# Ten SwiGLU pairs from seven products, with the sums of weights made by GpSimd beside them

## The chip, the cores and the metric

The kernel runs on one core of a Trainium2 chip. The metric is the device time of one execution in microseconds: 818.55 is the median of three runs (817.93 to 819.12). Five engines work side by side, each on its own list of instructions in a fixed order: TensorE (PE, with its weight loads as PEld), VectorE (DVE), ScalarE (ACT), GpSimd (POOL) and SyncE (SP). SP issues nearly all the loads and stores here.

## The reference

A decoder block on 512 tokens of width 1024, all in float32. What matters here:

```python
h = rmsnorm(x, norm1_g)
z = h @ w_in + b_in                     # 1024 -> 2048 + 1280 + 1280 + 1024 + 1024
...                                     # conv branch y_a, gated recurrence y_b
m = sigmoid(z_ga) * y_a + sigmoid(z_gb) * y_b
x = x + m @ w_mix_out
h = rmsnorm(x, norm2_g)
x = x + (silu(h @ ffn_w1) * (h @ ffn_w3)) @ ffn_w2      # width 2816 between
return rmsnorm(x, norm_f_g)
```

The recurrence has two block-diagonal products (lru_wa and lru_wx, 16 heads of 80 channels).

## The kernel before

Activations lie with channels on the 128 partitions and tokens (512) along the row. To keep float32 accuracy on TensorE, each operand is split into a high and a low part, and a product is three matmuls: high x high, high x low, low x high. For a weight chunk of 128x1024 the split is a copy on ScalarE (line 118) and a subtraction (line 114): on GpSimd for the input stage's weights, on VectorE for all later ones.

**Weights.** `wchunk` lists the chunks in the order in which they are used; `emit_chunk` issues a chunk's load into one of four raw tiles and its split into one of five hl tiles; `weights(key, ahead)` emits up to four chunks beyond the one asked for. So a split can begin when the product five chunks earlier has ended.

**Stages.** Input stage (products z, gates g, the two branches; GpSimd splits its weights), products yb and ya, the mixing product (mxr), norm 2, the SwiGLU stage (f and fr), the last product (or) with the final norm. The Tile framework orders each engine's instructions when the kernel is compiled, from the order of the program text; inside `manual_schedule` the order of the text is kept. `issue_after(ins)` puts a block's instructions on `ins`'s engine behind `ins`.

**Products from seven.** A product that is cut into 2x2 quarters on each side can be made from seven quarter products instead of eight, from sums of the inputs' quarters and of the weights' quarters (b11, b12, b21, b22 and the sums t1 = b12 - b11, t2 = b22 - b12 + b11, t3 = b22 - b12, t4 = b21 - t2). `Sevenfold` does so for the mixing product and the last product. In the SwiGLU stage a pair k is the output tiles k and k + 11 of both w1 and w3. Before, pairs 2 to 6 (`SEVEN`) come from seven products (`ffn_seven`, 168 matmuls of 256 columns), the other six are plain (96 matmuls of 512).

**Sums of weights.** For pairs 2 to 6, `make_f_sums` runs in the input stage: 20 blocks, each with four loads, four GpSimd instructions of 128x256 and four stores to device memory. The SwiGLU stage loads the sums back. For the last product `make_sums` runs in the SwiGLU stage on VectorE: 11 blocks, each with two loads, four VectorE instructions of 128x512 and four stores (`out_sums`).

**Beside norm 2.** The first plain pair (tiles 0 and 11) is begun on the first 256 tokens while the second 256 are normalised, then finished on the second. `turn_half` makes h2's halves: transposes on TensorE, the high part on ScalarE, the low part on VectorE. `f_inputs` makes the seven products' inputs from h2: eight additions high + low on GpSimd, sixteen sums of 128x256 and eight splits on VectorE. `pair` does the same for the last product's input, after each pair k.

**Gates and ext.** A gate chunk j loads pieces of lru_wa and lru_wx, one DMA for each piece of each. The channels of a head that lie in the neighbouring tile come by way of `ext`: parts of xb's split tiles, copied by DMA (`ext_in`, line 698).

Of the kernel before, what the change touches and what calls it, by code (L numbers as in the profile page):

```python
# [44 lines left out]
SEVEN = (2, 3, 4, 5, 6)  # L45
SUMS_AT, SUMS_STEP, SUMS_LAG, STORE_LAG = 4, 3, 2, 5
# [35 lines left out]
def tile_block(ctx, tc, a, out):  # L82
# [53 lines left out]
    def emit_chunk():  # L136
# [3 lines left out]
        raw = raws.tile([P, 1024], F32, tag="raw", name=f"raw_{key}")  # L140
        rv = raw[:, :n]
        if callable(src):
# [3 lines left out]
        if where == "hl":  # L146
# [30 lines left out]

    gate_view = lambda v: v.rearrange("p (g e n) -> p g e n", g=2, e=2)

    def gate_chunk(j):  # L180
        main, runs, blocks = pieces[j % 5]

        def load(raw):
            pool_e.memset(raw[:, :512], 0.0)
            v = gate_view(raw[:, :512])
            for gi, name in enumerate(("lru_wa", "lru_wx")):
                for ei, blk in ((0, main), (1, blocks)):
                    for r, nr, c, ncol, h, hr, hc in blk:
                        nc.sync.dma_start(v[r : r + nr, gi, ei, c : c + ncol], a[name][0, h + 8 * (j // 5), hr : hr + nr, hc : hc + ncol])
# [34 lines left out]
    dram = ctx.enter_context(tc.tile_pool(name="dram", bufs=1, space=bass.MemoryType.DRAM))  # L224

    class Quartered:
        def __init__(self, name, w, kh, lo, parts=()):
# [3 lines left out]
            self.sums = {(n, k): dram.tile([P, T], F32, tag=f"{name}{n}_{k}", name=f"{name}{n}_{k}") for n in ("t1", "t2", "t3", "t4") if n not in parts for k in range(kh)}  # L231
            self.at = {}

            def quarter(n, k):
                if n[0] == "t":
                    return self.sums[n, k][:, :]
                i, h = int(n[1]) - 1, int(n[2]) - 1
                return w[:, k + kh * i, h * T : (h + 1) * T]
# [11 lines left out]
            for p_ in (("b11", "t1", "b21"), ("t2", "t3", "b22"), ("t4",)):  # L250
                p_ = [n for n in p_ if n not in parts]
                for k in range(kh):
                    if len(p_) % 2 and k % 2 == 0:
                        chunk(f"{p_[-1]}_{k}", [(p_[-1], i) for i in (k, k + 1) if i < kh])
                    if len(p_) > 1:
                        chunk(f"{p_[0]}_{k}", [(n, k) for n in p_[:2]])

# [19 lines left out]
        def make_sums(self, k):  # L277
# [8 lines left out]
            for n, v in (("t1", q12), ("t2", q11), ("t3", q22), ("t4", q21)):  # L286
                if n in self.parts:
                    self.parts[n][k] = split(f"{self.name}{n}{k}", v, vec)
                else:
                    nc.sync.dma_start(self.sums[n, k][:, :], v)  # L290
# [7 lines left out]
    f_sums = {(n, k): dram.tile([P, 1024], F32, tag=f"f{n}_{k}", name=f"f{n}_{k}") for k in SEVEN for n in ("t1", "t2", "t3", "t4")}  # L298

# [5 lines left out]
    def f_chunk(n, k):  # L305
        def load(raw_t):
            if n[0] == "t":
                nc.sync.dma_start(raw_t, f_sums[n, k][:, :])
            else:
                for i, w_ in enumerate((w1, w3)):  # L310
                    nc.sync.dma_start(raw_t[:, i * T : (i + 1) * T].rearrange("p (k n) -> p k n", k=4), f_quarter(n, k, w_, 0, 4))

        wchunk(f"f{n}_{k}", load, 8, P, lo=vec)

    def make_f_sums():

        todo = [(k, i, c) for k in SEVEN for i in range(2) for c in (0, 2)]
        sums_due, stores_due = [], []  # L320
        n = 0
        while todo or sums_due or stores_due:
            if stores_due and emitted[0] >= stores_due[0][0]:
                stores_due.pop(0)[1]()
            if sums_due and n >= sums_due[0][0]:
                sums_due.pop(0)[1]()
            if todo and n >= SUMS_AT and (n - SUMS_AT) % SUMS_STEP == 0:
                k, i, c = todo.pop(0)
                raw = wsums.tile([P, 1024], F32, tag="wsum", name=f"fws{k}_{i}_{c}")
                q = [raw[:, 256 * m : 256 * m + 256] for m in range(4)]  # L330
                with tc.issue_after(newest["load"]):
                    for m, v in zip(("b11", "b12", "b21", "b22"), q):
                        nc.sync.dma_start(v.rearrange("p (k n) -> p k n", k=2), f_quarter(m, k, (w1, w3)[i], c, c + 2))

                def sums(q=q, k=k, at=T * i + P * c):
                    q11, q12, q21, q22 = q
# [6 lines left out]
                    def stores():  # L343
                        with tc.issue_after(newest["load"]):
                            for m, v in (("t1", q12), ("t2", q11), ("t3", q22), ("t4", q21)):
                                nc.sync.dma_start(f_sums[m, k][:, at : at + 256], v)

                    stores_due.append((emitted[0] + STORE_LAG, stores))

                sums_due.append((n + SUMS_LAG, sums))  # L350
            n += 1
            yield

    for k in range(KF):
        if k in SEVEN:
            for n in ("b11", "b21", "b22", "t2", "t1", "t3", "t4"):
                f_chunk(n, k)
        else:
            for j in (k, k + KF):
                wchunk(f"f1_{j}", w1[:, :, j * P : (j + 1) * P], ND, P, lo=vec)  # L360
                wchunk(f"f3_{j}", w3[:, :, j * P : (j + 1) * P], ND, P, lo=vec)
    outq = Quartered("o", a["ffn_w2"][0].rearrange("(k p) n -> p k n", p=P), NF // 2, vec)
# [147 lines left out]
    with tc.manual_schedule(engines={ET.PE, ET.Activation, ET.DVE, ET.SP}):  # L510
# [248 lines left out]
    f_sums_steps = make_f_sums()  # L759
    for kind, j in ORDER:  # L760
        next(f_sums_steps, None)
# [20 lines left out]
    for j in range(8):  # L782
# [5 lines left out]
        next(f_sums_steps, None)  # L788
# [4 lines left out]
    for _ in f_sums_steps:  # L793
# [366 lines left out]
```

## Time and profile before

| | |
|---|---|
| median of 3 runs | 818.55 us |
| span of the profiled execution | 817.8 us |
| granted TensorE clock, mean | 0.997 |
| TensorE's last matmul of the SwiGLU stage begins | 703.6 us |
| HBM | read 127.13 MB, written 28.31 MB |

The span is from the first to the last instruction of one profiled execution; its times are in microseconds from the span's start. In a group's row stand the line, the engine, the operation, the output and inputs by the program's names, the shape and the count, then busy us and the mean ns of one, then the engine's idle time before them and what ended it. In a timeline's row stand start, length, engine, line and what it does. A matmul's length is longer than its share of time, since matmuls overlap; what one costs is read from the starts of a run of them.

### The profile page before, as it was taken

How to read it: one execution, taken by the hardware profiler on the slowest of the kernel's cores; microseconds unless marked ns; L12 is line 12 of the kernel's file. 1: busy time of each engine (PE TensorE's matmuls, PEld its weight loads, DVE VectorE, ACT ScalarE, POOL GpSimd, SP SyncE). 2: the span in 40 equal slices, each digit the busy share in tenths (PEclk: the TensorE clock that was granted, in tenths of full speed). 3: DMA queues.
4: the chain of work that ended last, by engine and by line, in shares of the span. 5: the costliest groups of instructions: out<-in, count | busy, mean ns of one | idle time of the engine just before them, and what ended most of it. 6: DMA issues, size and time to landing. Idle time of an engine off the chain costs nothing.

```text
span 817.8 us, 11826 instructions
## 1 busy us (share of the span) xinstructions
PE 800.2 (98%) x4110; PEld 685.3 (84%) x4110; DVE 654.9 (80%) x1018; ACT 448.4 (55%) x633; POOL 225.3 (28%) x172
## 2 busy tenths in 40 slices
PE   8999999899999999999999999999999999999996
PEld 7988888678888888888888898999998888788885
DVE  4699899989989988787878869787877565779556
ACT  7546585977668855553336455364644222466443
POOL 3575766866765854000000042000000000000000
PEclk9999999999999999999999999999999999999999
DMA  6746466477675753456838524788787887796552
GB/s 195 206 127 163 128 172 201 125 191 201 180 207 166 210 177 113 126 169 217 262 117 245 155 92 149 249 251 268 227 238 207 272 266 266 277 316 206 180 168 103
DMA packets 189551, 159.25 MB, mean 195 GB/s; under 512 B 14407, under 2 KB 157171, under 8 KB 189491
## 3 DMA queue, kind: packets, MB, share of 16 engines
q1 hardware_dynamic: 189491, 158.50, 63.5%
q8 instruction: 32, 0.52, 0.3%
q14 instruction: 28, 0.23, 0.1%
HBM read 127.13 MB, written 28.31 MB: 190 GB/s over the span
## 4 chain that ended last, share of the span: by engine, by line
PE 68%; DVE 12%; DMA 10%; SPq 3%; ACT 3%; issue 2%; POOL 2%; DVEq 0%; POOLq 0%; ACTq 0%
PE z L438 24%; PE or L841 12%; PE fr L1017 9%; PE yb L438 7%; PE ya L438 5%; PE mxr L841 5%; PE f L438 4%; DVE cv L597 3%; DMA ows<-in_ffn_w_dram 3%; DMA raw_in<-in_w_in_dram 2%; DMA ot<-ows 2%; PE g L718 1%; DVE hl_f L114 1%; POOL hl_in L114 1%; DVE ows L114 1%
## 5 line engine op out<-in xcount | busy, mean ns | idle before, releaser
L597 DVE SCALAR_TENSOR_TENSOR cv<-u,par,cv 128x511 f32<-128x511 f32 (+16 forms) x240 | 162.4, 730 | 2.4 <-ACT cv L594 2.2
L114 POOL TENSOR_TENSOR hl_in<-raw_in,hl_in 128x1024 fp32r<-128x1024 f32 x52 | 125.6, 2422 | 81.2 <-ACT hl_in L118 80.3
L118 ACT CAST hl_in<-raw_in 128x1024 fp32r<-128x1024 f32 x52 | 54.2, 1043 | 10.9 <-PE z L438 6.5
L114 POOL TENSOR_TENSOR fws<-fws 128x256 f32<-128x256 f32 x60 | 47.8, 799 | 5.0 <-DMA fws<-in_ffn_w_dram 2.3
L991 POOL TENSOR_TENSOR hf<-h20h,h20l 128x512 f32<-128x512 f32 x1 | 1.3, 1271 | 163.5 <-DVE h20l L482 163.5
L118 ACT CAST hl_f<-raw_f 128x1024 fp32r<-128x1024 f32 x24 | 25.1, 1051 | 36.3 <-DMA raw_f<-in_ffn_w_dram 14.9
L438 PE MATMUL z<-h10h,hl_in 128*128 128x512 f32 (+1 forms) x112 | 42.6, 382 | 1.1 <-DVE h10l L482 0.6
L438 PE MATMUL z<-h11h,hl_in 128*128 128x512 f32 (+1 forms) x112 | 41.7, 374 | 0.0
L438 PE MATMUL z<-h16h,hl_in 128*128 128x512 f32 (+1 forms) x112 | 41.7, 374 | 0.0
L438 PE MATMUL z<-h13h,hl_in 128*128 128x512 f32 (+1 forms) x112 | 41.7, 374 | 0.0
L438 PE MATMUL z<-h14h,hl_in 128*128 128x512 f32 (+1 forms) x112 | 41.7, 374 | 0.0
L438 PE MATMUL z<-h15h,hl_in 128*128 128x512 f32 (+1 forms) x112 | 41.7, 374 | 0.0
L438 PE MATMUL z<-h17h,hl_in 128*128 128x512 f32 (+1 forms) x112 | 41.7, 374 | 0.0
L438 PE MATMUL z<-h12h,hl_in 128*128 128x512 f32 (+1 forms) x112 | 41.7, 374 | 0.0
L114 DVE TENSOR_TENSOR hl_ob<-raw_ob,hl_ob 128x1024 fp32r<-128x1024 f32 (+1 forms) x23 | 26.9, 1176 | 17.8 <-ACT hl_ob L118 17.7
L118 ACT CAST hl_ob<-raw_ob 128x1024 fp32r<-128x1024 f32 (+1 forms) x23 | 23.3, 1015 | 31.7 <-PE or L841 12.0
L114 DVE TENSOR_TENSOR hl_f<-raw_f,hl_f 128x1024 fp32r<-128x1024 f32 x24 | 32.9, 1380 | 9.5 <-ACT hl_f L118 9.4
L114 DVE TENSOR_TENSOR ows<-ows,ows 128x512 f32<-128x512 f32 x22 | 15.2, 690 | 19.6 <-DMA ows<-in_ffn_w_dram 15.3
L1017 PE MATMUL fr<-hs_0h,hl_ft 128*128 128x256 f32 x160 | 29.7, 284 | 0.9 <-ACT c L1029 0.9
L114 DVE TENSOR_TENSOR hl_ft<-raw_ft,hl_ft 128x1024 fp32r<-128x1024 f32 x20 | 24.4, 1219 | 5.3 <-ACT hl_ft L118 5.3
L114 DVE TENSOR_TENSOR hl_ot<-raw_ot,hl_ot 128x1024 fp32r<-128x1024 f32 (+1 forms) x17 | 20.1, 1190 | 10.6 <-ACT hl_ot L118 10.2
L438 PEld LDWEIGHTS z<-h10h,hl_in 128*128 128x128 f32 x112 | 21.4, 191 | 5.8 <-DVE h10l L482 0.9
(903 smaller groups left out, 2602.5 us busy)
## 6 DMA issues: line engine op xcount, KB each, us to landing
raw_in<-in_w_in_dram SPq DMA_DIRECT2D x52, 512.0 KB
raw_f<-in_ffn_w_dram SPq DMA_DIRECT2D x24, 512.0 KB
ows<-in_ffn_w_dram SPq DMA_DIRECT2D x22, 512.0 KB
ot<-ows SPq DMA_DIRECT2D x44, 256.0 KB
fws<-in_ffn_w_dram SPq DMA_DIRECT2D x80, 128.0 KB
ft<-fws SPq DMA_DIRECT2D x80, 128.0 KB
raw_ft<-ft SPq DMA_DIRECT2D x20, 512.0 KB
raw_ob<-in_ffn_w_dram SPq DMA_DIRECT2D x33, 256.0 KB
```

The lines of the kernel that those rows point to most:

```text
L114: return eng.tensor_tensor(out=o, in0=x, in1=y, op=ALU.subtract)
L118: copy(h, full)
L438: pe.matmul(ps, l, r, start=i == 0, stop=i == n - 1)
L597: vec.scalar_tensor_tensor(out=acc[c][:, s:], in0=u[c][:, : T - s], scalar=dw(c, s), in1=acc[c][:, s:], op0=ALU.mult, op1=ALU.add)
L718: pe.matmul(ps, l, r, start=k == 0, stop=k == len(mms) - 1)
L841: pe.matmul(banks[i], l_[:, ts], r_, start=start and n == 0, stop=stop and n == 2, skip_group_check=again)
L991: pool_e.tensor_tensor(out=v, in0=h2p[c][0].bitcast(F32), in1=h2p[c][1].bitcast(F32), op=ALU.add)
L1017: pe.matmul(ps[:, HALVES[i]], lw[:, 4 * i + c, :], rx_, start=not (again or i or c or m), stop=bool(i and c == 3 and m == 2), skip_group_c ...
```

## The change

- In the SwiGLU stage, pair 0 is plain and pairs 1 to 10 come from seven products. Each loads its four quarters (b11, b21 into the raw tiles, b12, b22 into the two wsums tiles), and GpSimd makes t1 to t4 in place, four subtractions of 128x1024: t1 when its chunk is emitted, t2, t3 and t4 after b22's split. The sums take no way through device memory.
- Beside norm 2, pairs 1 and 2 are begun: their first two products need only the first 256 tokens. They are finished after pair 0; for that b11, b12 and b21 are loaded again.
- `f_inputs` makes its eight additions on VectorE instead of GpSimd.
- The last product's sums of weights are made in the input stage by GpSimd: 22 blocks, each with two loads, four instructions of 128x256 and one store. `out_sums` is gone from the SwiGLU stage.
- `pair` of the last product is run for pairs 0 to 3 in the SwiGLU stage, and for 4 to 10 three steps ahead in the first loop of `Sevenfold.run`.
- The gate weights are first copied, device memory to device memory, into one tensor with lru_wa and lru_wx side by side; a gate chunk's piece of both then comes in one DMA.
- ext for gate tiles 0 and 5 is made by two ScalarE copies and one VectorE subtraction from xb instead of by DMA from the split parts.

```diff
-SEVEN = (2, 3, 4, 5, 6)
-SUMS_AT, SUMS_STEP, SUMS_LAG, STORE_LAG = 4, 3, 2, 5
+PLAIN, FIRST = 0, (1, 2)
+EARLY_SUMS, SUMS_AHEAD = 4, 3
+SUMS_AT, SUMS_STEP, SUMS_LAG, STORE_LAG = 4, 3, 2, 4
...
+    def load_gates():
+        for gi, name in enumerate(("lru_wa", "lru_wx")):
+            nc.sync.dma_start(gate_rows[:, gi, :], a[name][0].rearrange("h r n -> (h r) n"))
...
-            for gi, name in enumerate(("lru_wa", "lru_wx")):
-                for ei, blk in ((0, main), (1, blocks)):
-                    for r, nr, c, ncol, h, hr, hc in blk:
-                        nc.sync.dma_start(v[r : r + nr, gi, ei, c : c + ncol], a[name][0, h + 8 * (j // 5), hr : hr + nr, hc : hc + ncol])
+            for ei, blk in ((0, main), (1, blocks)):
+                for r, nr, c, ncol, h, hr, hc in blk:
+                    at_ = HB * (h + 8 * (j // 5)) + hr
+                    nc.sync.dma_start(v[r : r + nr, :, ei, c : c + ncol], gate_rows[at_ : at_ + nr, :, hc : hc + ncol])
...
+    def f_load(n, k):
+        p_, tag = (wsums, "wsum") if n in ("b12", "b22") else (raws, "raw")
+        raw = p_.tile([P, 1024], F32, tag=tag, name=f"raw_f{n}_{k}")
+        for i, w_ in enumerate((w1, w3)):
+            nc.sync.dma_start(raw[:, i * T : (i + 1) * T].rearrange("p (k n) -> p k n", k=4), f_quarter(n, k, w_, 0, 4))
+        f_raw[n, k] = raw
+        return raw
+
+    def f_sum(n, k):
+
+        q11, q12, q21, q22 = (f_raw.get((m, k)) for m in ("b11", "b12", "b21", "b22"))
+        o, x, y = {"t1": (q12, q12, q11), "t2": (q22, q22, q12), "t3": (q11, q22, q11), "t4": (q21, q21, q22)}[n]
+        sub(pool_e, o, x, y)
+        f_raw[n, k] = o
+
+    F_ORDER = ("b11", "b21", "t1", "b22", "t2", "t3", "t4")
+    F_LOADS = {"b11": ("b11", "b12"), "b21": ("b21",), "b22": ("b22",)}
...
+        def after(rv, h):
+            for m in ("t2", "t3", "t4"):
+                f_sum(m, k)
+
+        wchunk(f"f{n}_{k}", source, 8, P, "made", vec, after if n == "b22" else None)
...
+    for k in FIRST:
+        f_chunk("b11", k, False)
+        f_chunk("b21", k, False)
+    plain_chunks(PLAIN)
+    for k in range(KF):
+        if k != PLAIN:
+            for n in F_ORDER[2 if k in FIRST else 0 :]:
+                f_chunk(n, k, True if k in FIRST else None)
...
+    def make_out_sums():
+
+        todo = [(k, c) for k in range(KF) for c in (0, 256)]
...
+        load_gates()
         early_mm(0, 0)
         early_mm(1, 0)
         turn_half("tx", xt, "norm1_g", h1p, 1, [bank2, bank, bank])
...
+                if j5 == 0:
+                    full, e = xb[i][:FEW, :], ext[key][0]
+                    act.copy(e[:FEW, :], full)
+                    act.copy(e[2 * FEW : 3 * FEW, :], full)
+                    sub(vec, e[FEW : 2 * FEW, :], full, e[:FEW, :].bitcast(F32))
+                    continue
...
             for k in range(kh):
+                for kk in range(min(kh, k + 1 + SUMS_AHEAD)):
+                    self.pair(kk)
...
-    for hf in range(2):
-        if hf:
-            turned = turn_half("th", xs, "norm2_g", h2p, 1, [bank2])
-        for i in range(EARLY):
-            for w_, p_ in zip(wf[i], pf[i]):
-                mm3(p_[:, HALVES[hf]], w_, parts_of(h2p, HALVES[hf]))
+    first = {}
+    for k in FIRST:
+        first[k] = bank(f"fr1_{k}"), bank(f"fr2_{k}")
+        for i, (ps, w_) in enumerate(zip(first[k], ("b11", "b21"))):
+            f_product(ps, k, parts_of(h2p[4 * i : 4 * i + 4], HALVES[0]), w_, ahead=0)
+    turned = turn_half("th", xs, "norm2_g", h2p, 1, [bank2])
     h2 = parts_of(h2p)
     with tc.issue_after(turned):
         emit_to(emitted[0] + 3)
...
             for v, c in ((a1, k), (a2, k + 4)):
-                pool_e.tensor_tensor(out=v, in0=h2p[c][0].bitcast(F32), in1=h2p[c][1].bitcast(F32), op=ALU.add)
+                add(v, h2p[c][0].bitcast(F32), h2p[c][1].bitcast(F32))
...
+    for k in FIRST:
+        begun(k, *first[k])
+    for j in (PLAIN, PLAIN + KF):
+        p1, p3 = bank(f"f1_{j}"), bank(f"f3_{j}")
+        mm3(p1, w_tiles(f"f1_{j}", ND), h2)
+        mm3(p3, w_tiles(f"f3_{j}", ND), h2)
+        ffn_out(j, p1, p3)
...
+        product(r5, "s1", "t1")
         product(r3, "s4", "b22")
         product(r1, "s2", "t2", True)
         q = shortt(f"q_{k}")
         act.copy(q, r1)
-        product(r5, "s1", "t1")
...
+    for k in range(KF):
+        if k != PLAIN:
             ffn_seven(k)
-            out_sums(k % 2)
-            continue
...
+        if k < EARLY_SUMS:
+            o7.pair(k)
```

More of the change, by code (lines that the diff above doesn't have):

```diff
@@ L303, in f_quarter @@
         return w_[:, c + c0 : c + c1, j * P : (j + 1) * P]
[L305 to L320 removed]
+    f_raw = {}
@@ L331, in make_f_sums @@
                 with tc.issue_after(newest["load"]):
[L332 to L336, printed above, removed]
+                    for i in range(2):
+                        nc.sync.dma_start(
+                            raw[:, 512 * i : 512 * i + 512].rearrange("p (h n) -> p h n", h=2),
+                            outq.w[:, k + KF * i, :].rearrange("p (h n) -> p h n", h=2)[:, :, c : c + 256],
+                        )
@@ L341, in sums, with store @@
                         sub(pool_e, q21, q21, q11)
[L343 to L348, printed above, removed]
+                def store(raw=raw, k=k, c=c):
+                    with tc.issue_after(newest["load"]):
+                        nc.sync.dma_start(
+                            outq.sums[k][:, :].rearrange("p (m n) -> p m n", m=4)[:, :, c : c + 256],
+                            raw.rearrange("p (m n) -> p m n", m=4),
+                        )
                 sums_due.append((n + SUMS_LAG, sums))
+                sums_due.append((n + STORE_LAG, store))
             n += 1
             yield
[L354 to L362, printed above, removed]
     x2_kept = [[dram.tile([P, T], F32, tag=f"x2k{t}{h}", name=f"x2k{t}{h}") for h in range(2)] for t in range(NT)]
@@ L953, in tile_block @@
     o7 = Sevenfold(outq)
-    sums_of = iter(range(KF))
-    def out_sums(n):
-        with tc.issue_after(turned):
-            for _ in range(n):
-                k = next(sums_of, None)
-                if k is not None:
-                    outq.make_sums(k)
     def ffn_out(j, p1, p3):
```

147 lines of the change are left out of this document (86 added, 61 removed).

## The prediction

> **What bounds the kernel now.** I read the page's busy times first, then the waits of TensorE, then busy times by stretch, then the chain of waits.
>
> ```profile
> span 817.8 us, 11826 instructions
> PE 800.2 (98%) x4110; PEld 685.3 (84%) x4110; DVE 654.9 (80%) x1018; ACT 448.4 (55%) x633; POOL 225.3 (28%) x172
> ...
> PE g L718 <- DMA ext<-xb6h: 4.3, 1, 4.3
> PE or L841 <- DVE ov L967: 1.3, 1, 1.3
> ...
> PE fr L1017 <- ACT c L1029: 0.9, 1, 0.9
> ```
>
> TensorE is busy 98% of the span, and its waits are few: one of 4.3 us in the input stage and two small ones. So a gain has to come from less TensorE work, and a loss from any engine that can no longer keep ahead of it. The second question is how far VectorE and GpSimd are from that in the SwiGLU stage (columns: the stretch, its length, then PE, PEld, DVE, ACT and POOL busy us).
>
> ```profile
> 479.00:485.40 6.40, 6.05 (x47) 5.42 (x46) 3.57 (x9) 3.55 (x8) 3.10 (x3) 1.00 0.01 3
> ...
> 545.00:617.00 72.00, 72.00 (x601) 72.00 (x601) 59.30 (x88) 39.84 (x57) 0.00 (x0) 1.00 0.80 243
> 617.00:704.00 87.00, 87.00 (x385) 72.03 (x384) 50.08 (x79) 25.32 (x34) 0.00 (x0) 1.00 0.78 251
> ```
>
> With seven products a pair (545 to 617) VectorE is busy 59.3 of 72 us and GpSimd not at all; with plain pairs (617 to 704) VectorE is busy 50.1 of 87.
>
> **TensorE's work.** The chain of waits (start, length, engine and line) gives the price of a matmul from long unbroken runs.
>
> ```profile
> 252.51 65.30 PE z L438 x288
> ...
> 467.44 11.51 PE f L438 x96
> ...
> 544.71 72.26 PE fr L1017 x600
> ```
>
> A 512-column matmul costs 65.30/288 = 0.227 us, a 256-column one 72.26/600 = 0.120. A plain pair is 96 of the first, 21.8 us; a pair from seven products 168 of the second, 20.2. Two halves do not cost one whole, so the saving is 1.5 us a pair and not the eighth that the count of operations suggests. Before: 192 halves for the first pair (23.0), five plain pairs (108.8), five of seven (101.1): 232.9 us. After: one plain (21.8) and ten of seven (202.3): 224.1. Minus 8.8 us.
>
> **The cover beside norm 2.** Both kernels do 96 half matmuls while the second token half is normalised. Before, the first pair's second halves then filled the time in which h2 was turned.
>
> ```profile
> 478.79 0.60 PE L478 MATMUL th<-ident,xs 128*128 128x128 f32 x4
> ...
> 484.99 0.48 DVE L482 SCALAR_TENSOR_TENSOR h27l<-th,par,h27h 128x256 fp32r<-128x256 f32 x1
> 485.39 4.03 DVE L114 TENSOR_TENSOR hl_f<-raw_f,hl_f 128x1024 fp32r<-128x1024 f32 x2
> ```
>
> After, nothing is left to multiply there: the plain pair needs its first chunk's low part, and that VectorE subtraction stands behind the last h27l by the issue_after. TensorE then has only transposes from 478.8 until 485.4 + 1.2 = 486.6. From there 21.8 us of plain pair and 1584 halves (190.7) end at 699.1, against 704.1 now (544.71 + 72.26 + 384 x 0.227): minus 5.0 instead of minus 8.8. That is the best end for the stage, and it holds if VectorE always keeps ahead.
>
> **VectorE and GpSimd.** The sums move to GpSimd beside the products, four of 128x1024 a pair. The input stage shows what happens when VectorE subtracts or adds two SBUF tiles while GpSimd works.
>
> ```profile
> 110.63 2.40 POOL L114 TENSOR_TENSOR hl_in<-raw_in,hl_in 128x1024 fp32r<-128x1024 f32 x1 [4.29 <-ACT hl_in L118]
> ...
> 111.62 1.96 DVE L114 TENSOR_TENSOR xb4l<-xb,xb4h 128x512 fp32r<-128x512 f32 x1
> ...
> 484.81 1.29 POOL L991 TENSOR_TENSOR hf<-h21h,h21l 128x512 f32<-128x512 f32 x1
> 486.06 2.28 POOL L991 TENSOR_TENSOR hf<-h25h,h25l 128x512 f32<-128x512 f32 x1
> 488.29 2.28 POOL L991 TENSOR_TENSOR hf<-h22h,h22l 128x512 f32<-128x512 f32 x1
> ```
>
> The VectorE split xb4l (0.68 us alone) took 1.96: it ended 0.55 after GpSimd's subtraction did, at 113.03. From 485.39 on both engines had such work, and one VectorE split with one GpSimd 512-wide addition took 2.28 together, while the GpSimd addition just before, alone for most of its time, took 1.29. The two engines take turns. So GpSimd's time counts against VectorE's, and I sum both. Prices: VectorE's issue-to-issue times in the seven-product stretch (576.33, 576.93, 578.07, 578.40), and GpSimd's mean of 52.
>
> ```profile
> 576.33 0.68 DVE L797 TENSOR_TENSOR q<-fr,q 128x512 f32<-128x512 f32 x1
> 576.93 1.22 DVE L114 TENSOR_TENSOR hl_ft<-raw_ft,hl_ft 128x1024 fp32r<-128x1024 f32 x1
> 578.07 0.42 DVE L1024 TENSOR_TENSOR ov<-q 128x256 f32<-128x256 f32 x1
> 578.40 0.69 DVE L797 TENSOR_TENSOR c<-fr,c 128x512 f32<-128x512 f32 x1
> ...
> L114 POOL TENSOR_TENSOR hl_in<-raw_in,hl_in 128x1024 fp32r<-128x1024 f32 x52 | 125.6, 2422 | 81.2 <-ACT hl_in L118 80.3
> ...
> L114 POOL TENSOR_TENSOR fws<-fws 128x256 f32<-128x256 f32 x60 | 47.8, 799 | 5.0 <-DMA fws<-in_ffn_w_dram 2.3
> ```
>
> 512 wide 0.60 us, 1024 wide 1.14, 256 wide 0.33; GpSimd 1024 wide 2.4. VectorE from 485.4 to the last split:
> - 70 weight splits (4 plain, 5 each for the two pairs begun, 56): 79.8
> - f_inputs, with its eight additions moved here from GpSimd: 8 x 0.60 + 16 x 0.33 + 8 x 0.60 = 14.9
> - 50 additions out of PSUM: 30.0
> - 44 products of 256: 14.5
> - pair() for four pairs, 0.60 + 5 x 0.33 each: 9.0
>
> In all 148, of which 147 ahead of the last split. That alone fits into 213 us. GpSimd adds 40 x 2.4 = 96 to it: 243. What counts is how much of a GpSimd sum VectorE waits out. Upper bound: all, 2.4. Lower: each sum hides behind one of the 50 additions that read PSUM (0.60) and behind the switch between engines (1.14 + 1.29 - 2.28, about 0.15), so 1.6 to 1.7. I take 1.9: the additions are a fifth of VectorE's time, so few sums meet one, but ScalarE's copies now and then leave VectorE idle. Then the last split ends at 485.4 + 147 + 76 = 708.4, and with the last product (24 x 0.120 = 2.9) the stage at 711.3: 7.2 us later than now. The make_sums of ows that leaves VectorE (44 x 0.60 = 26 us) was mostly in the plain pairs, where there was room.
>
> Loads in this stage shrink. A pair from seven products read 3.5 MB and now reads 2 (the two begun pairs 1.5 more, as three quarters are read again), and the reads and writes of make_sums for ffn_w2 (2 MB a block, eleven blocks) are gone. TensorE waited for no load there, so I count nothing for it. One wait is new on SP: b12 and b22 have two buffers, wsums, so b22's load waits until the pair before has made t4 from its tile, and behind it on SP stand the next pair's b11, b12 and b21. They are used 7 products (20 us) after; a load lands in about 5, as the raw_in row below shows.
>
> The Trainium skill ("SBUF — State Buffer", Who interferes with whom) has it that a VectorE instruction with two SBUF inputs and a GpSimd instruction that reads SBUF exclude each other for the whole instruction. By that alone every sum would cost 2.4, and the time would be the second rival's; the turns above, 0.15 shorter than their sum, bear most of it out.
>
> **The input stage.** GpSimd makes 22 blocks of sums instead of 20, 8 more instructions of 0.8 us (the fws row), beside work with which it already waits 80 us for ScalarE. Three DMA issues a block replace eight, and two gate blocks come in one DMA. Against that, load_gates puts two DRAM copies on SP's queue ahead of the fourth weight chunk.
>
> ```profile
> 17.93 4.66 DMA raw_in<-in_w_in_dram
> 22.59 0.02 issue
> 22.61 1.05 ACT hl_in L118
> 23.67 0.07 issue
> 23.73 2.41 POOL hl_in L114
> ...
> q1 hardware_dynamic: 189491, 158.50, 63.5%
> ...
> GB/s 195 206 127 163 128 172 201 125 191 201 180 207 166 210 177 113 126 169 217 262 117 245 155 92 149 249 251 268 227 238 207 272 266 266 277 316 206 180 168 103
> ```
>
> TensorE uses that chunk at 23.7, with no slack. The copies are 2560 rows of 320 bytes, 0.82 MB. No row has such a copy. At the queue's mean packet, 63.5% x 817.8 x 16 / 189491 = 0.044 us, they take 7.0 us of 16 engines; at the 300 GB/s that the page's fastest slices move, 2.7. I take 4, with 1 us for two issues: plus 5.
>
> ```profile
> 157.39 2.31 SPq L189 DMA_DIRECT2D raw_gate<-in_lru_wa_dram  x5
> 159.74 1.04 SPq L189 DMA_DIRECT2D raw_gate<-in_lru_wx_dram  x2
> 160.89 0.54 SPq L698 DMA_DIRECT2D ext<-xb6h  x1
> ...
> 164.18 0.76 PE L718 MATMUL g<-ext,hl_gate 96*128 96x512 f32 x1 [4.31 <-DMA ext<-xb6h]
> ```
>
> The 4.3 us wait is for an ext copy that stood behind seven gate loads on SP. After, ScalarE and VectorE make this ext from xb, about 0.6 us each, and the wait goes: minus 4.3, or nothing, if VectorE, near full there, is late next. The stage gives plus 0.7 (minus 1.6 to plus 8).
>
> **The last product.** TensorE's 1.3 us wait for ov was for the last pair; it goes, as that pair is now made three steps ahead. Pairs 4 to 10 (7 x 2.25 = 15.8 us) move into the first loop, 11 x 18 x 0.227 = 45 us long.
>
> ```profile
> 730.00:740.00 10.00, 10.00 (x46) 8.29 (x45) 8.85 (x12) 7.38 (x12) 0.00 (x0) 1.00 0.70 212
> ...
> 760.00:770.00 10.00, 10.00 (x46) 8.29 (x45) 4.90 (x4) 3.37 (x4) 0.00 (x0) 1.00 0.62 182
> ```
>
> VectorE is at 88% there and at half in the loop after. Chunks four ahead and pairs three ahead give some 11 us of slack, which covers the excess; I count nothing, and 6 us if the cover is gone.
>
> **Sum.** 7.2 - 1.3 + 0.7 = plus 6.6. The profiled span is 817.8 and the median of the runs 818.55; the difference is put on the median: 825.2.
>
> **Rivals.**
> - TensorE stays the bound. GpSimd's sums hide under additions from PSUM and VectorE's idle time. For it: VectorE has 213 us for 147. Against: the sum of both is 243. It decides below 1.74 us a sum, where the terms cancel; with nothing left over, -5.0 - 1.3 + 0.7 = -5.6: 813.0. Faster.
> - Every sum blocks in full, 2.4: 20 us more than the forecast, 845. For it: xb4l above. Against: the 0.15 a turn, and VectorE's idle time.
> - The first loop of the last product turns VectorE-bound as well: 831. For it: 88% busy before 15.8 us are added. Against: the slack.
> - The sums don't arrive: b22's load, its split, three sums in a row and t4's split, 2.3 + 7.2 + 2.3 = 12 us after the load, have seven products (20 us) from slot to use. If GpSimd's chain were the bound the time would be as in the second rival; it is held in that chance.
>
> **Numbers.** A difference under 0.2% can't be told from none. Forecast 0.48 (820 to 834), the first rival 0.27, full blocking 0.14, the last product 0.11. Most of the first rival is faster by over 0.2%: 0.25; its edge and the forecast's give 0.05 for no change; slower 0.70. The range leaves out a part of both outer rivals: 812 to 841, the forecast's own 820 to 834.
>
> **What would show it.** In the changed profile, VectorE's splits of the chunks hl_fb and hl_ft beside a GpSimd sum should last 2 to 3.5 us instead of 1.22, VectorE should be near 100% busy from 485 to the end of the SwiGLU stage, and TensorE should wait there for those splits, most between 505 and 560, where f_inputs and the five-product pairs fall together. TensorE should idle about 6 us before the plain pair, lose about 5 near 24 us, and not wait for ext. Unbroken TensorE in the pairs after the third would make the forecast wrong towards the first rival; waits for GpSimd itself, or for loads, would make its reason wrong.

## The result: 842.7 us, and the profile after

| | before | after |
|---|---|---|
| median of 4 runs | 818.84 us (817.93 to 819.94) | 842.69 us (841.81 to 844.83) |
| ratio after / before | | 1.030 (95% interval 1.0285 to 1.0315) |
| span of the profiled execution | 817.8 us | 841.1 us |

The change makes the kernel 3% slower. The forecast had the sign and the kind of loss (VectorE kept busy by sums that GpSimd makes). But it gave a loss of 6.6 us where the loss is 23.3 us of span, and its range ended at 841. The top of the page of the changed kernel:

```profile
span 841.1 us, 12219 instructions
...
PE 800.5 (95%) x4374; PEld 694.7 (83%) x4374; DVE 728.3 (87%) x1024; ACT 471.4 (56%) x677; POOL 330.9 (39%) x212
```

TensorE has as many busy microseconds as before (800.5 against 800.2), although its products should take 8.8 us less: it waits more, and for some microseconds its matmuls are slower, as shown below. VectorE is busy 73 us more. To place the loss I cut the span at two starts of TensorE's matmuls: the first of the 96 half matmuls beside norm 2, and the first of the last product (`or`). The two starts before, then after:

```profile
467.28 0.28 PE L438 MATMUL f<-h20h,hl_f 128*128 128x256 f32 x1
703.87 0.39 PE L841 MATMUL or<-hl_ob,ous0h 128*128 128x512 f32 x1
```

```profile
472.76 0.28 PE L1030 MATMUL fr<-h20h,hl_fb 128*128 128x256 f32 x1
726.90 0.40 PE L904 MATMUL or<-hl_ob,ous0h 128*128 128x512 f32 x1
```

| | before | after | difference |
|---|---|---|---|
| up to the half matmuls beside norm 2 | 467.28 | 472.76 | +5.5 |
| from there to the first `or` (the SwiGLU stage) | 236.6 | 254.1 | +17.5 |
| from there to the end | 113.9 | 114.2 | +0.3 |

**The SwiGLU stage.** TensorE's four largest waits in it, in the changed kernel (us in total, times, longest; two more come to 1.4):

```profile
PE fr L1030 <- ACT q L1106: 7.2, 8, 2.2
PE fr L1030 <- ACT hs_0h L119: 7.1, 3, 3.3
PE fr L1030 <- DVE hl_ft L115: 4.2, 4, 1.5
PE fr L1030 <- DVE hs_0l L115: 1.2, 1, 1.2
```

They are waits for the inputs of the products (hs), for weight splits (hl_ft), and for ScalarE's copy q out of a bank to which the next product adds. None is for GpSimd or for a load. Busy times by stretch, in the stretches of the prediction. The first stretch before (the prediction has the other two), then all three after:

```profile
485.00:545.00 60.00, 59.12 (x407) 55.13 (x406) 52.85 (x84) 31.14 (x44) 11.48 (x6) 1.00 0.66 206
```

```profile
485.00:545.00 60.00, 50.30 (x301) 43.96 (x302) 55.08 (x70) 23.56 (x38) 23.95 (x9) 0.94 0.30 85
545.00:617.00 72.00, 63.20 (x514) 61.78 (x514) 67.86 (x71) 31.37 (x48) 33.08 (x13) 1.00 0.32 91
617.00:704.00 87.00, 84.24 (x691) 83.03 (x691) 75.73 (x69) 42.58 (x61) 43.04 (x16) 1.00 0.36 106
```

TensorE idles 9.7, 8.8 and 2.8 us. VectorE is at 92 and 94% in the first two and at 87% in the last.

The third number from the end is TensorE's granted clock, as a share of full speed: 0.94 in the first stretch, where the kernel before has 1.00. The clock stands at 0.50 from 515.9 to 522.7 us, among TensorE's longest waits, and its 256-column matmuls there start 0.213 us apart instead of 0.120. By these starts, the 17 matmuls in it cost about 1.6 us more.

The timeline of one late pair shows how VectorE and GpSimd share the time; first VectorE:

```profile
625.24 0.68 DVE L857 TENSOR_TENSOR c<-fr,c 128x512 f32<-128x512 f32 x1
628.71 2.45 DVE L115 TENSOR_TENSOR hl_ft<-raw_fb,hl_ft 128x1024 fp32r<-128x1024 f32 x1 [2.78 <-ACT hl_ft L119]
631.08 2.62 DVE L1078 TENSOR_TENSOR ov<-c 128x256 f32<-128x256 f32 x1
633.74 2.51 DVE L115 TENSOR_TENSOR oe<-ou,ov 128x256 f32<-128x256 f32 x1
636.17 1.21 DVE L115 TENSOR_TENSOR hl_ft<-raw_fb,hl_ft 128x1024 fp32r<-128x1024 f32 x1
```

and GpSimd in the same microseconds:

```profile
625.12 10.84 POOL L115 TENSOR_TENSOR raw_fb<-raw_fb,raw_fb 128x1024 f32<-128x1024 f32 x4 [10.46 <-DVE hl_fb L115]
```

While GpSimd makes four sums in a row (10.84 us), VectorE first idles 2.78 us, since the next chunk to split is the sum being made, and then three instructions take 2.45, 2.62 and 2.51. Two of them are 256 wide and take 0.42 elsewhere. Each lasts about as long as one sum (2.4), whatever its own width. The addition c, which reads PSUM, takes its usual 0.68 under the first sum. The Trainium skill ("SBUF — State Buffer", Who interferes with whom) says that a VectorE instruction with two SBUF inputs and a GpSimd instruction that reads SBUF contend, and that one with at most one SBUF input, outside the modes that use both ports, does not. These rows agree (2.45 to 2.62 us against 0.68).

**The input stage.** The chain of waits at the place of the new copies of the gate weights:

```profile
17.83 1.30 SPq L190
19.17 6.27 DMA raw_in<-in_w_in_dram
25.47 1.05 ACT hl_in L119
26.56 4.54 PE z L491 x24
```

The load of the fourth weight chunk was issued at 17.93 and took 4.66; now it is issued 1.2 us later and takes 6.27. TensorE waits 3.1 us for that chunk (0.3 before), and its clock stands at 0.50 from 27.8 to 31.2 us. At the ext place, TensorE's waits between 155 and 200 us are now three:

```profile
PE z L491 <- DVE xb L802: 2.4, 1, 2.4
PE g L778 <- DVE ext L115: 1.2, 1, 1.2
PE g L778 <- DVE y1l L115: 0.8, 1, 0.8
```

The one wait of 4.3 us for a transfer has become 4.4 us of waits for VectorE. The clock stands at 0.50 among them for 6.8 us (from 167.7), where it did for 3.4 us before (from 164.0, behind the one wait). By the starts of the matmuls at half clock, an estimate, the input stage loses about 2 us more to them than before. One of VectorE's rows there, beside a GpSimd weight split:

```profile
161.96 2.81 DVE L115 TENSOR_TENSOR ext<-xb,ext 32x512 fp32r<-32x512 f32 x1
```

The new subtraction on 32 partitions takes 2.81 us and not the 0.6 that I took, because it stands behind hl_in (161.85, 2.37 us) on GpSimd: it ends 0.55 after it.

### The profile page after: what moved, and what is told of

Read it like the earlier page. It is cut to its first block, busy times and chain, and to the rows that moved or that the text cites. A ratio compares the mean times of both kernels' runs of the same rounds, so it can differ in the third digit from the quotient of the medians.

```text
span 841.1 us, 12219 instructions
## 1 busy us (share of the span) xinstructions
PE 800.5 (95%) x4374; PEld 694.7 (83%) x4374; DVE 728.3 (87%) x1024; ACT 471.4 (56%) x677; POOL 330.9 (39%) x212
## 4 chain that ended last, share of the span: by engine, by line
PE 57%; DVE 26%; issue 5%; ACT 4%; DMA 3%; POOL 2%; SPq 1%; DVEq 0%; POOLq 0%; ACTq 0%
PE z L491 27%; PE or L904 7%; PE yb L491 6%; DVE hl_ft L115 6%; PE ya L491 5%; PE mxr L904 5%; PE fr L1030 4%; DVE cv L651 3%; DVE hl_fb L115 2%; POOL raw_fb L115 2%; PE g L778 2%; DMA raw_in<-in_w_in_dram 2%; DVE ov L1078 1%; DVE hl_ob L115 1%; DVE q L857 1%
## 5 line engine op out<-in xcount | busy, mean ns | idle before, releaser
L115 POOL TENSOR_TENSOR raw_fb<-raw_fb,raw_fb 128x1024 f32<-128x1024 f32 x40 | 107.5, 2706 | 241.1 <-DMA raw_fb<-in_ffn_w_dram 122.1
L115 DVE TENSOR_TENSOR hl_ft<-raw_fb,hl_ft 128x1024 fp32r<-128x1024 f32 x40 | 67.9, 1698 | 16.6 <-ACT hl_ft L119 16.6
L119 ACT CAST hl_ft<-raw_fb 128x1024 fp32r<-128x1024 f32 x40 | 42.0, 1050 | 55.8 <-POOL raw_fb L115 53.5
L115 POOL TENSOR_TENSOR ows<-ows 128x256 f32<-128x256 f32 x66 | 57.4, 871 | 37.5 <-DMA ows<-in_ffn_w_dram 34.5
L1030 PE MATMUL fr<-hs_0h,hl_ft 128*128 128x256 f32 x320 | 62.9, 287 | 7.1 <-ACT hs_0h L119 7.1
L1030 PEld LDWEIGHTS fr<-hs_0h,hl_ft 128*128 128x128 f32 x320 | 52.4, 194 | 7.9 <-ACT hs_0h L119 7.8
L1030 PE MATMUL fr<-hs_0l,hl_ft 128*128 128x256 f32 x160 | 46.0, 287 | 1.2 <-DVE hs_0l L115 1.2
L115 DVE TENSOR_TENSOR hl_fb<-raw_fb,hl_fb 128x1024 fp32r<-128x1024 f32 x30 | 36.0, 1219 | 3.0 <-ACT hl_fb L119 2.9
L119 ACT CAST hl_fb<-raw_fb 128x1024 fp32r<-128x1024 f32 x30 | 30.7, 1044 | 9.1 <-PE f L491 5.4
L1030 PE MATMUL fr<-hs_1h,hl_ft 128*128 128x256 f32 x160 | 31.4, 286 | 4.4 <-DVE hl_ft L115 4.2
L119 ACT CAST hl_ob<-raw_ob 128x1024 fp32r<-128x1024 f32 (+1 forms) x23 | 23.3, 1015 | 20.6 <-PE or L904 15.1
```

Source lines behind the costliest of these rows:

```text
L115: return eng.tensor_tensor(out=o, in0=x, in1=y, op=ALU.subtract)
L119: copy(h, full)
L1030: pe.matmul(ps[:, HALVES[i]], lw[:, 4 * i + c, :], rx_, start=not (again or i or c or m), stop=bool(i and c == 3 and m == 2), skip_group_c ...
```

## Experiments

All kernels were timed beside the kernel before, in jobs in which that took 818.6 to 819.6 us. "Stage" is the SwiGLU stage as cut above, from each kernel's profiled execution; the ratio is to the kernel before. e2 and e3 leave the sums out of the products and don't compute the block. e4 was timed twice (842.65 and 847.64), and its stage is from the longer of the two.

| kernel | median us | ratio (95% interval) | stage us |
|---|---|---|---|
| before | 818.84 | | 236.6 |
| after | 842.69 | 1.0285 to 1.0315 | 254.1 |
| e1, sums on VectorE | 825.19 | 1.0051 to 1.0091 | 236.1 |
| e2, no sums | 818.57 | 0.9974 to 1.0003 | 230.1 |
| e3, sums that nobody reads | 844.21 | 1.0275 to 1.0325 | 257.1 |
| e4, t1 later | 845.14 | 1.0269 to 1.0354 | 258.2 |
| e12, sums in halves | 843.49 | 1.0273 to 1.0313 | 252.0 |
| e5, gates apart | 838.85 | 1.0191 to 1.0281 | 254.2 |
| e6, gates apart, ext by DMA | 840.21 | 1.0209 to 1.0283 | 254.1 |
| e7 = e1 + e6 | 819.57 | 0.9984 to 1.0019 | 236.0 |
| e9 = e7, additions on GpSimd | 819.17 | 0.9978 to 1.0014 | 235.4 |
| e10 = e1 + e5 | 819.43 | 0.9987 to 1.0008 | 236.6 |
| e8 = e1, gates copied later | 820.19 | 0.9994 to 1.0016 | 236.2 |
| e13 = e10, two plain pairs | 813.04 | 0.9916 to 0.9943 | 228.6 |

**e1: the sums on VectorE.**

```diff
-        sub(pool_e, o, x, y)
+        sub(vec, o, x, y)
```

> The 40 sums of the SwiGLU stage made by VectorE instead of GpSimd, nothing else. Theory 'turns' (a GpSimd sum of 2.4 us keeps VectorE from its own two-SBUF work): VectorE then has 147 + 40 x 1.14 = 193 us of work in a stage that TensorE needs 213 for, with nobody to wait for, so 14 to 22 us go: 821 to 829. Rival 'VectorE has too much work': 46 us more on it, slower than the changed kernel's 842.7. Rival 'GpSimd's chain of sums is late': also faster, by what the chain costs (told apart by the two kernels that follow).

17.5 us come back with one word, and the time lies in the range of the turns. VectorE's groups in the SwiGLU stage of e1:

```profile
L115 DVE TENSOR_TENSOR hl_ft<-raw_fb,hl_ft 128x1024 fp32r<-128x1024 f32 x40 | 48.3, 1220 | 0.0
L115 DVE TENSOR_TENSOR raw_fb<-raw_fb,raw_fb 128x1024 f32<-128x1024 f32 x40 | 48.0, 1220 | 0.2
```

A sum takes VectorE 1.22 us by itself. On GpSimd, it takes GpSimd 2.71 in the mean and costs VectorE more than that 1.22, as worked out below. Here the off-loading costs the engine that it was to relieve more than the work itself.

**e2: no sums at all.** The same line is taken out, so the four t chunks are split from the loaded quarters.

> The 40 sums are left out; the four t chunks of a pair are split straight from the loaded quarters. All theories: the stage without the price of sums, 820 to 824. What is left above 818.8 is the input stage's 5.5 us and the gap after norm 2.

This is what the stage would take if the sums cost nothing: 230.1, 6.5 us less than before. The time, 818.57, lies under the 820 to 824 that was expected. It also gives VectorE's own work. From behind h27l to the end of the last split, the sum of the stretches up to 605 us and from there (columns as above), first of e2 and then of the changed kernel:

```profile
sum 198.90, PE 196.64 PEld 192.63 DVE 150.26 ACT 101.27 POOL 0.00; mean PE 98.32 PEld 96.31 DVE 75.13 ACT 50.63 POOL 0.00
```

```profile
sum 229.17, PE 208.46 PEld 201.22 DVE 210.61 ACT 101.70 POOL 106.15; mean PE 104.23 PEld 100.61 DVE 105.31 ACT 50.85 POOL 53.08
```

VectorE's 229.2 us are 150.3 of its own work, 60.3 by which instructions beside sums are longer (1.5 a sum) and 18.6 in which it idles, 16.6 of them for ScalarE's copies of hl_ft, which wait for a sum. Together a sum costs VectorE (229.2 - 150.3) / 40 = 2.0 us. The same difference for e1, where VectorE is busy 190.3 us with the sums in it, gives (190.3 - 150.3) / 40 = 1.0 us a sum: instructions that follow each other without a gap overlap a little. For the same reason the 150.3 of e2, where VectorE often idles, is a little high as its own work in the changed kernel, and the 2.0 a little low.

**e3: sums that nobody reads.** GpSimd does the same 40 subtractions into b12's tile, and the chunks t1 to t4 are split from raw quarters.

```diff
-        sub(pool_e, o, x, y)
-        f_raw[n, k] = o
+        sub(pool_e, q12, x, y)
+        f_raw[n, k] = {"t1": q11, "t2": q22, "t3": q11, "t4": q21}[n]
```

> GpSimd makes the 40 sums as before, but into b12's tile, and no split reads them: the t chunks are split from the loaded quarters. 'Turns': as slow as the changed kernel but for a few us, 834 to 842. 'Chain late': as fast as without sums, 820 to 824.

The time stays, 2 us above the range of the turns and 20 above that of a late chain. So the loss doesn't need a product that waits for a sum: it is enough that GpSimd works. The stretch from 605 us to VectorE's last split in e3:

```profile
605.00:720.20 115.20, 113.01 (x931) 111.82 (x930) 114.92 (x98) 55.90 (x81) 60.42 (x21) 1.00 0.33 96
```

VectorE is busy 114.9 of 115.2 us; the idle time is gone, and other instructions are longer instead. In e3's groups:

```profile
L115 DVE TENSOR_TENSOR hl_fb<-raw_fb,hl_fb 128x1024 fp32r<-128x1024 f32 x26 | 56.4, 2192 | 0.0
L1078 DVE TENSOR_TENSOR ou<-c 128x256 f32<-128x256 f32 x20 | 25.9, 1301 | 0.0
```

hl_fb is 1.22 and ou<-c 0.42 in e1, and 2.19 and 1.30 here. In the changed kernel the same waiting stands in other groups, hl_ft 1.70 and ov<-c 2.38:

```profile
L115 DVE TENSOR_TENSOR hl_ft<-raw_fb,hl_ft 128x1024 fp32r<-128x1024 f32 x40 | 67.9, 1698 | 16.6 <-ACT hl_ft L119 16.6
...
L1078 DVE TENSOR_TENSOR ov<-c 128x256 f32<-128x256 f32 x9 | 21.4, 2377 | 0.0
```

**e12: each sum in two halves.** If a short instruction loses by waiting out a whole long one, shorter sums should help.

```diff
-        sub(pool_e, o, x, y)
+        for c in (slice(0, T), slice(T, 2 * T)):
+            sub(pool_e, o[:, c], x[:, c], y[:, c])
```

> The changed kernel with each GpSimd sum in two instructions of half the width, 128x512. If VectorE and GpSimd take turns and VectorE stands still for as long as GpSimd works, 80 sums of 1.2 us block as much as 40 of 2.4 and the time stays within 2 us of 842.7. If the loss is that a short VectorE instruction waits out a whole long sum (rounding up), it falls by a third or so of the 17.5 us, to 836 or 838. If the sums cost through their own length on the chain of chunks, GpSimd's extra instruction makes it a little slower, 844.

No gain in the time (the stage is 2.1 us shorter, the stretches before and behind it each 1.7 longer). GpSimd's group and the largest wait of VectorE in the stage:

```profile
L115 POOL TENSOR_TENSOR raw_fb<-raw_fb,raw_fb 128x512 f32<-128x512 f32 x80 | 131.9, 1684 | 217.7 <-DMA raw_fb<-in_ffn_w_dram 121.2 <-DVE hl_fb L115 66.1 <-ACT c L1114 21.8
```

```profile
DVE hl_ft L115 <- ACT hl_ft L119: 37.3, 19, 2.9
```

VectorE's instructions wait less, but GpSimd now waits too (131.9 us, where 80 of the shortest half, 1.28, are 102), the sums come later, and VectorE idles 37.3 us for them instead of 16.6. From its first plain split to its last split VectorE needs 235.1 us here, 235.6 in e3, 235.7 in the changed kernel. Three forms of the same waiting come to the same stretch within 0.7 us.

**e4: t1's chunk and product behind t2, as in the kernel before.** The named wait for q could mean that the new order of the products is at fault.

```diff
-    F_ORDER = ("b11", "b21", "t1", "b22", "t2", "t3", "t4")
+    F_ORDER = ("b11", "b21", "b22", "t2", "t1", "t3", "t4")
...
-            for m in ("t2", "t3", "t4"):
+            for m in ("t1", "t2", "t3", "t4"):
```

> The t1 product is put back behind the t2 product, so that two products instead of one (2.9 us) lie between t2 and t4, which adds to the same PSUM bank that ScalarE copies to q in between. If the order is to blame for the 7.2 us that TensorE waited for that copy: 834 to 837. 'Turns' alone: VectorE is the bound, the wait moves to another place, 840 to 844.

It doesn't help: TensorE's wait for q falls from 7.2 us to 0.6, and a wait of 11.4 for another copy of ScalarE's (c, line 1069 of its kernel) takes its place. So the wait for q is a symptom. In the changed kernel GpSimd makes the sums four in a row (t2, t3 and t4 with the next pair's t1); here, from the second pair on, it makes mostly three and one. That is no better either.

**e5 and e6: the input stage undone, part by part.** e5 loads the gate pieces as before (`load_gates` gone); e6 also takes the new ext code out, so that all of ext comes by DMA.

```diff
-        load_gates()
...
```

> Of the change only the copy of the gate weights into one tensor is undone: each piece of each gate matrix is loaded by its own DMA again. Theory 'the copies delay the fourth weight chunk': TensorE's wait near 23 us (3.4 us in the changed kernel) goes, and with it 3 to 4 us: 838.5 to 840. Rival 'VectorE sets the input stage's end': the start is earlier, the wait near 163 us longer by as much: 842 to 844. Rival 'more DMA issues on SP bring a wait back': 843 to 846.

```diff
-                if j5 == 0:
-                    full, e = xb[i][:FEW, :], ext[key][0]
...
-                    sub(vec, e[FEW : 2 * FEW, :], full, e[:FEW, :].bitcast(F32))
-                    continue
```

> As the kernel just before, and ext for gate tiles 0 and 5 comes by DMA again. If making ext on ScalarE and VectorE cost as much as the wait that it removed (5.9 us of waits near 163 us against 4.3): 1 to 2 us less than the kernel just before, 837 to 838.5. If it was a gain: 1 to 4 us more.

The copies cost 3.8 us here, and 5.8 with the sums on VectorE (825.19 in e1, 819.43 in e10). The two don't differ beyond the spread: the four runs of e5 lie between 837.74 and 840.84, and the spans of the profiled executions give 4.8 (841.1 and 836.3) and 4.1 (822.9 and 818.8). Making ext on the engines is worth nothing that can be measured: 838.85 and 840.21 have overlapping intervals, and so have 819.43 and 819.57 (e10, e7). e6 has the old wait again:

```profile
PE g L764 <- DMA ext<-xb6h: 5.4, 1, 5.4
```

**e8: the copies of the gates later,** with the sums on VectorE.

```diff
-        load_gates()
         early_mm(0, 0)
         early_mm(1, 0)
         turn_half("tx", xt, "norm1_g", h1p, 1, [bank2, bank, bank])
         emit_to(4)
+        load_gates()
```

> The sums on VectorE, and the copies of the gate weights issued behind the chunks of the early products, not ahead of them. If the copies cost time only because the input's next rows of weights queue behind them, the 3.8 us come back and the time is that of the kernel with the gates loaded apart, 818 to 821.5. If the copies cost time wherever they stand, since the gate chunks wait for them, it stays at 824 to 826.

825.19 becomes 820.19, where no copies give 819.43: the loss came from the place on SP's queue, ahead of a load with no slack, and not from the copies themselves.

**e7, e9 and e10: combinations.** e7 is e1 with e6's edits, e10 is e1 with e5's. e9 is e7 with the eight additions of f_inputs on GpSimd again:

```diff
-                add(v, h2p[c][0].bitcast(F32), h2p[c][1].bitcast(F32))
+                pool_e.tensor_tensor(out=v, in0=h2p[c][0].bitcast(F32), in1=h2p[c][1].bitcast(F32), op=ALU.add)
```

> Sums of the SwiGLU stage on VectorE, and gates and ext as in the kernel before. If the two costs add: 825.2 - 5.5 = 819.7, 818 to 821, no difference from the kernel before that can be told. If VectorE is the bound of the stage from 515 us on, the earlier start is kept all the same, since its work starts earlier too. Below 817 would mean that the costs hide each other.

> As the kernel just before, with the eight additions of f_inputs on GpSimd again, the rest of GpSimd's SwiGLU work left with VectorE. 'Turns': eight additions of 1.27 us keep VectorE off for about as long, against 8 x 0.60 that it saves: 3 to 6 us slower, where TensorE waits for hs (5 to 7 us in the changed kernel): 822 to 826. Rival 'VectorE has too much work there': faster by up to 5 us, 814 to 818.

> The sums on VectorE and the gate weights loaded apart, the block-diagonal input made on the engines as in the changed kernel. If the parts add up as the earlier runs have them (sums on VectorE 825.2, copies of the gates 3.8 of it, the input made on the engines worth about 1.4), the time is 821.4; with the last product's own gain found in the runs with the old input stage (819.6, there with the 5 us wait for the transferred input), it is about 818, at or just under the kernel before. If the making of the block-diagonal input costs the VectorE stage what the wait gave, it is 819.6 again.

All three equal the kernel before within 0.2%. For e9 the turns had 3 to 6 us more, and that did not come. The contention is in its trace (three subtractions of 128x256 take 1.5 us each beside the additions, and 0.42 in e7). But VectorE is spared the eight additions, and its last split of f_inputs starts only 1.0 us later than in e7 (517.80 and 516.76).

So with the sums on VectorE and the gates undone, the ten pairs still win nothing, though TensorE has less to do. Where that goes shows in the time of each pair on TensorE, worked out from the starts of its fr matmuls (the two begun pairs need 120 x 0.120 = 14.4 us, the others 20.2):

| pair | 1 | 2 | 3 | 4 | 5 | 6 | 7 | 8 | 9 | 10 |
|---|---|---|---|---|---|---|---|---|---|---|
| after | 25.8 | 18.4 | 23.3 | 22.9 | 21.6 | 21.3 | 21.0 | 21.0 | 21.0 | 20.2 |
| e2 | 17.7 | 14.4 | 20.2 | 20.2 | 20.2 | 20.2 | 20.2 | 20.2 | 20.2 | 20.2 |
| e10 | 24.3 | 14.4 | 20.2 | 20.2 | 20.2 | 20.2 | 20.2 | 20.2 | 20.2 | 20.2 |

In e10 one pair loses 9.9 us, the first; in the changed kernel that one loses 11.4 and the nine others 14.7. TensorE's waits in e10's first pair:

```profile
PE fr L1022 <- ACT hs_0h L119: 2.7, 2, 1.8
PE fr L1022 <- DVE hs_0l L115: 0.9, 1, 0.9
PE fr L1022 <- DVE hl_ft L115: 0.9, 1, 0.9
PE fr L1022 <- DVE hs_1l L115: 0.7, 1, 0.7
```

They are for the products' inputs, which VectorE makes in f_inputs among splits and sums, and come to 5.2 of the 9.9 us. Most of the rest is the clock. The stretch in which e10's clock is halved, and starts of matmuls in it and behind it:

```profile
512.86:523.10 10.24, 7.76 (x35) 7.24 (x34) 8.12 (x19) 2.70 (x4) 0.00 (x0) 0.50 0.16 46
```

```profile
520.24 0.41 PE L1022 MATMUL fr<-hs_0l,hl_ft 128*128 128x256 f32 x1
520.45 0.41 PE L1022 MATMUL fr<-hs_0h,hl_ft 128*128 128x256 f32 x1
...
523.29 0.28 PE L1022 MATMUL fr<-hs_1h,hl_fb 128*128 128x256 f32 x1
523.41 0.28 PE L1022 MATMUL fr<-hs_0l,hl_ft 128*128 128x256 f32 x1
```

33 matmuls run at half clock, 0.21 us apart instead of 0.12; that is 3 to 4 us, and each restart behind a wait costs about 0.1 to 0.3 more. So short waits cost nearly twice their length here. In the SwiGLU stage of e2 and e13 the clock is full throughout. That the waits bring the clock down was not tested by itself. In the changed kernel and in e10 the stretch begins behind several waits in a row.

**e13: a second plain pair as cover.** e10 with pairs 0 and 1 plain, 2 and 3 begun beside norm 2, nine pairs from seven products.

```diff
-PLAIN, FIRST = 0, (1, 2)
+PLAIN, FIRST = (0, 1), (2, 3)
...
-    plain_chunks(PLAIN)
+    for k in PLAIN:
+        plain_chunks(k)
...
-        if k != PLAIN:
+        if k not in PLAIN:
...
-    for j in (PLAIN, PLAIN + KF):
+    for j in [j for k in PLAIN for j in (k, k + KF)]:
```

> Sums on VectorE, gate weights loaded apart, and two plain pairs ahead of the others (pairs 0 and 1 plain, 2 and 3 begun beside norm 2, nine pairs from seven products). With one plain pair the first pair from seven products takes 24 us on TensorE where it needs 14.4, as its inputs and its sums come together on VectorE (17.7 without the sums). If VectorE's lateness is in that place alone, the second plain pair (21.8 us with little for VectorE) covers it: it costs 1.5 us more of TensorE's work and four sums fewer, and up to 9 us of waits go, so 812 to 815 us, faster than both kernels. If the first 20 us behind norm 2 are bound by VectorE whatever stands there, the waits move to the next pair and the time is 819 to 821.

813.04 us, ratio 0.9929: faster than both kernels. In e13 and e10, the stretch in which f_inputs run:

```profile
505.00:525.00 20.00, 20.00 (x90) 16.56 (x89) 19.76 (x35) 9.21 (x13) 0.00 (x0) 1.00 0.23 67
```

```profile
505.00:525.00 20.00, 14.79 (x84) 13.51 (x83) 17.59 (x32) 7.57 (x11) 0.00 (x0) 0.74 0.27 79
```

VectorE is as full as it can be (19.76 of 20), but TensorE has the plain pair to do meanwhile, its clock stays full (1.00 against 0.74), and every later pair takes its 14.4 or 20.2.

## Why the prediction was right and where it fell short

**Right.** TensorE would be the loser and VectorE the cause; the two engines take turns on SBUF; the sums cost more than the saved matmuls give; no wait for GpSimd itself or for loads. The best end of the stage, 5.0 us less than before if VectorE kept ahead, is borne out by e2 (6.5 less). The copies of the gates at plus 5 were measured at 3.8 to 5.8. The price of a sum, taken as 1.9 between 1.6 and 2.4, is 2.0 or a little more.

**The step that failed is the sum for the SwiGLU stage: "the last split ends at 485.4 + 147 + 76 = 708.4 ... the stage at 711.3: 7.2 us later than now".** It measured 17.5. The terms were too small, all in one direction:
- from h27l to the last split, 223.0 forecast and 229.2 measured: 2.9 of the 6.2 from the sums (78.9 against 76), the other 3.3 from VectorE's own work (150.3 against 147; with less own work, as said at e2, the sums' part is larger);
- from the last split to the stage's end, 2.9 forecast. The last split starts at 719.6 and takes 1.2, the first `or` at 726.9: 6.1, plus 3.2. TensorE then still had 50 matmuls to do (50 x 0.120 = 6.0), and not the 24 of one product;
- from norm 2's half matmuls to the end of h27l 0.8 more than before.

These are 10.2 of the 10.3 us. Behind it stands a way of counting that did not hold: one total for VectorE over the stage, set against its end, with TensorE one product behind it. From 703.8 us to the stage's end TensorE waits for nothing, so VectorE's last split does not set the end; what was lost earlier does. 15.4 us are lost in the first two pairs, where the slack of later ones can't be used, and about 1.6 of them by TensorE's halved clock, for which the forecast had no term. After that the pairs lose 3.1, 2.7, 1.4, 1.1, three times 0.8, and the last none, with VectorE at 88% from 605 us: GpSimd's sums come in one burst a pair, and first the idle 2.78 us and then three stretched instructions stand in it. The forecast had VectorE near 100% to the end of the stage; it is at 94% even up to 605 us.

**Rivals.** 845 for "every sum blocks in full" is nearest to the time, but by other terms: it put all of its 20 us more on a price of 2.4 for each sum. The price is 2.0, which gives 2.9 of them; the rest came from the terms above and from the input stage, so that its closeness is luck. "TensorE stays the bound" would have come close for sums that cost nothing: e2 gives 818.6 with the copies of the gates in it; without those 3.8 to 5.8 us it would be 812.8 to 814.8, where the rival had 813.0. That was not run. The last product did not turn VectorE-bound (113.9 and 114.2).

**The input stage: plus 0.7 forecast, plus 5.5 measured.** The term for the ext wait, minus 4.3, was taken whole; the text had the alternative beside it, "nothing, if VectorE, near full there, is late next", and that is what came: 4.4 us of waits for xb, ext and y1l in place of 4.3. With that term at nothing the forecast would have been plus 5.0. The waits give 2.9 of the 5.5 (3.1 against 0.3, 4.4 against 4.3), and matmuls at half clock about 2 more, again a term that the forecast did not have.

**The last product: minus 1.3 forecast, plus 0.3 measured.** The wait for ov is gone, but TensorE now waits 1.0 for ous10l and 0.6 for x2b. With 10.3 and 4.8 this gives the whole difference: 6.6 + 10.3 + 4.8 + 1.6 = 23.3.

**Said of the profile.** Splits beside sums 2 to 3.5 us: 2.1 to 3.4 for the 13 of 70 that met one, and the usual 1.2 for the others; the rest of the waiting stands in shorter instructions. VectorE near 100% busy: 92, 94 and 87%. Between 505 and 565 us TensorE idles 11.8 of the 21.3 us that it idles from 485 to 727, and nearly all the rest lies in the later pairs. Idle before the plain pair: it did not idle 6 us at a stretch; its first matmuls run among the transposes, as one low part of a chunk was ready before h27l (485.08).

Two things stay open. Whether VectorE's idle time for late sums would cost anything without the stretched instructions can't be told apart here, since the one turned into the other in e3 and e12. And what the halved clock costs the changed kernel as a whole is not shown, since VectorE is nearly full where it stands.

## What to carry to other kernels

Before work goes from VectorE to GpSimd, look whether VectorE's instructions beside it read two SBUF tiles: then the off-loaded instruction costs VectorE nearly its whole length (2.0 us of 2.4 here), where doing it on VectorE costs 1.22. Eight additions of 128x512 came out even on either engine (e7 and e9). When an engine's total is counted against a stage's end, do it by the stretch: 10 us lost in a first pair, half of them waits and most of the rest slow matmuls behind the waits, were not regained in nine pairs with slack. A second plain pair put in that place, though dearer on TensorE, made the kernel 0.7% faster than the one before. A copy is judged by what stands behind it on its queue: issued behind one more load, the same two copies cost almost nothing.

## What was unexpected of the hardware

- A VectorE product of two 128x256 tiles lasted 2.6 us instead of 0.42 beside a GpSimd sum: the length of the wait is GpSimd's, not its own.
- Halving GpSimd's instructions didn't shorten the whole: 80 halves took GpSimd 131.9 us in place of 107.5 for 40 sums, and VectorE's instructions were stretched less (188.9 us busy against 210.6) but its idle time grew.
- An addition with one input from PSUM kept its time (0.68 us) beside a sum, and the eight additions of f_inputs cost the same on either engine (819.57 and 819.17).
- Waits of 0.7 to 1.8 us, five of them within 9 us, stood ahead of or within 10.2 us at half clock in e10: 9.9 us lost for 5.2 us of waits.
